# Every fourth wide weight split: the low part by an adding transfer instead of VectorE

## The chip, the cores and the metric

The kernel runs on one core of a Trainium2 chip. The metric is device microseconds for one execution; several executions are timed and their median is taken. TensorE (PE in the profile) multiplies, VectorE (DVE) and ScalarE (ACT) work on tiles in on-chip memory, GpSimd (POOL) does small side work, and SyncE (SP) issues loads from HBM.

## The reference, cut to what matters

A two-layer encoder over 256 tokens of width 1024. Each layer is a feed-forward block, a mixer (attention) and a second feed-forward block:

```python
def swiglu(h, w_gate, w_up, w_down):
    return (jax.nn.silu(h @ w_gate) * (h @ w_up)) @ w_down
...
    for layer in range(DEPTH):
        h = rms_norm(x, ffn1_norm[layer])
        x = x + 0.5 * swiglu(h, ffn1_w_gate[layer], ffn1_w_up[layer], ffn1_w_down[layer])
        h = rms_norm(x, mix_norm[layer])
        ...                       # even_mixer or odd_mixer
        h = rms_norm(x, ffn2_norm[layer])
        x = x + 0.5 * swiglu(h, ffn2_w_gate[layer], ffn2_w_up[layer], ffn2_w_down[layer])
    return rms_norm(x, final_norm)
```

All of it is float32. The feed-forward width is 2816, so the four blocks' gate, up and down matrices are most of the weights.

## The kernel before

**Two parts for every factor.** The matrix products run on a narrower float type (fp32r). Each weight tile `raw` is therefore split into a high part, `hi`, which is the weight rounded to that type, and a low part, `lo = raw - hi`, which is what the rounding dropped. The activations are split in the same way (`th`, `tl`). One product of a weight piece is three matmuls, in `mm`: activation high by weight high (L453), activation high by weight low (L454), activation low by weight high (L455). TensorE takes them in this order, so the low part is needed one matmul after the high part.

**Where parts are made.** ScalarE writes the high part from the raw tile (`high_part`, L461), VectorE subtracts and writes the low part (`low_part`, L464). A unit of work is a `Split`: a raw tile of 128 partitions by up to 1024 elements in two pieces (two column halves of one row block, or two row blocks of 512 or 384 columns). Its kinds are narrow (attention weights, one piece at a time), wide (most feed-forward weights, both pieces at once) and the sums of the Strassen-like products (`strassen`, `seven_gates`), which save one product in eight in some chunks and some down rows.

**Buffers.** Raw tiles of over 512 elements per partition come from a pool of three, filled by SP's loads in `load` (L366). High and low parts come from a pool of seven pairs. A pair is free when the last of its matmuls is done, and only then can ScalarE write the next high part into it.

**Stages.** The feed-forward blocks are stages 0, 2, 3 and 5. Each goes through six column chunks of 512 or 384: eight gate pieces for token tile 0, the same eight for token tile 1, then the up pieces likewise, and later the rows of the down matrix.

**What sets the order.** The order on each engine is written out by the program: it records instructions in the sequence in which Python issues them, and each engine runs its list in order. After each product `tick` runs waiting small tasks (SiLU, norms, transposes, each with a counted delay) and, at a rate set per stage, `supply`, which makes the next split's high part. `low` makes its low part at the next tick, or earlier when a product needs it. GpSimd's own list in the feed-forward blocks is nearly empty: two powers per stage (`rstd`, L473) that give the reciprocal root for the norm.

Of the kernel before, what the change touches and what calls it, by code (L numbers as in the profile page):

```python
# [12 lines left out]
AF = mybir.ActivationFunctionType  # L13
ALU = mybir.AluOpType
# [6 lines left out]
D = 1024  # L21
# [25 lines left out]
ODD_RATE = [0.51, 0.41, 0.51, 0.49, 0.51, 0.39, 0.49, 0.51]  # L47

HELD = 2

X_WAIT = 5
R_WAIT = 3
# [74 lines left out]
class Split:  # L127
# [3 lines left out]
    def __init__(self, raw, uses, first=False, narrow=False, kind="wp", then=None):  # L131
        self.raw, self.first, self.narrow, self.kind, self.then = raw, first, narrow, kind, then
        n = raw.shape[1]
        self.left = sum(uses[i % len(uses)] for i in range(n))
        self.parts, self.made = None, 0

    def step(self):

# [50 lines left out]
def pairs(stage):  # L189
    return [({"p": "plain", "s": "strassen"}[o[0]], int(o[1:])) for o in DOWN[stage].split()]  # L190
# [9 lines left out]
class Trunk:  # L200
# [4 lines left out]
    def __init__(self, ctx, tc, a, out):  # L205
        self.ctx, self.tc, self.nc, self.a, self.out = ctx, tc, tc.nc, a, out
        pool = lambda name, bufs, **kw: ctx.enter_context(tc.tile_pool(name=name, bufs=bufs, **kw))
        self.one = pool("one", 1)
        self.ph = None
        self.raw = pool("raw", RAWS)  # L210
        self.wp = pool("wp", FIT["wp"])

        self.two = pool("two", 2)
        self.acc = pool("acc", 1, space=PSUM)
        self.n = 0
        self.rate = RATE[0]
        self.tasks, self.last, self.last_v = [], [], [[], []]
        self.units, self.whole, self.queue, self.due, self.half = self.plan(), [], [], 0, None
        self.live = {kind: 0 for kind in FIT}

        self.hts = {}

# [65 lines left out]
    def plan(self):  # L288
# [16 lines left out]
        def ffn(n, l, stage):  # L305
# [15 lines left out]
            for i, (kind, pair) in enumerate(pairs(stage)):  # L321
                src = a[n + "_w_down"][l][2 * pair * P : 2 * (pair + 1) * P, :].rearrange("(k p) n -> p k n", p=P)
                uses = [2, 3 if stage == 5 and i >= len(pairs(stage)) - HELD else 2]
                yield [(slice(0, P), src)], 2, D, uses, "wide" if kind == "plain" else kind
# [31 lines left out]
    def load(self):  # L356
        unit = next(self.units, None)
        if unit is None:
            return
        pieces, nk, w, uses, kind = unit  # L360
        if nk * w > 512:
            raw = self.raw.tile([P, nk, w], F32, tag="raw", name=self.name("raw"))
        else:
            raw = self.t([P, nk, w], "raw", 2)
        for sl, src in pieces:
            self.nc.sync.dma_start(raw[sl], src)  # L366

        halves = lambda t: t.rearrange("p (a w) -> p a w", a=2)
        if kind == "strassen":
            self.coming(self.strassen(raw, halves))  # L370
        else:
            views = [halves(raw[:, k, :]) for k in range(nk)] if w == D else [raw[:, k : min(k + 2, nk), :] for k in range(0, nk, 2)]
            self.coming([Split(view, uses, n == 0, kind == "narrow") for n, view in enumerate(views)])

    def coming(self, splits):
        self.whole += splits
# [25 lines left out]
    def supply(self):  # L402

        self.low()
        if not self.whole:
            return
        split = self.whole[0]
        _, a, w = split.raw.shape
        if split.parts is None:
            if split.first:  # L410
                self.load()
            if split.kind == "wp":
                split.parts = [self.wp.tile([P, 2, 512], F32R, tag=n, name=self.name(n)) for n in ("hi", "lo")]
            else:
                split.parts = [self.t([P, 2, 512], n, FIT["sum"], F32R) for n in ("shi", "slo")]
            split.parts = [t[:, :a, :w] for t in split.parts]
            self.live[split.kind] += 1
        sl = slice(split.made, split.made + split.step())
        self.high_part(split.parts[0][:, sl], split.raw[:, sl])
        split.made = sl.stop  # L420
        self.half = (split, sl)
        if split.made == a:
            self.whole.pop(0)

# [204 lines left out]
    def ffn(self):  # L629
# [295 lines left out]
        order = [i for i, (kind, _) in enumerate(down) if kind == "strassen"]  # L925
        for i, (kind, pair) in enumerate(down[:-HELD]):
            if kind == "strassen":
# [10 lines left out]
        if self.next.n == 6:  # L938
            last = [self.t([P, 2, 512], "shi", FIT["sum"], F32R) for _ in range(NT)]
            self.last = [t.bitcast(F32).rearrange("p a w -> p (a w)") for t in last]  # L940
        held = [f for _, pair in down[-HELD:] for f in (2 * pair, 2 * pair + 1)]
        for f in held:
# [590 lines left out]
```

## Time and profile before

| | |
|---|---|
| Runs | 956.24, 956.25 and 956.81 us, median 956.25 us |
| Span of the profiled execution | 954.4 us, 1.85 us less than the median, which is the time around it |
| Instructions in the span | 13005 |
| VectorE's subtractions for low parts of weights (L464 `lo<-raw,hi`) | 388 in three sizes, 375.9 us busy |
| ScalarE's high parts (L461 `hi<-raw`) | 388, 320.5 us busy |
| Transfers | 171.65 MB, 180 GB/s mean |
| Transfers issued by GpSimd | none |

An engine's busy time is given with its share of the span; the idle time of an engine that nobody waits for costs nothing. TensorE's matmuls overlap their neighbours, so the time from one to the next is shorter than the duration in the row (some 0.23 us for 512 columns where the row says 0.39). In a timeline row stand the start, the time, the engine, the line, and what is written from what; x2 means two in a row, and a bracket holds the idle time before it and who ended it.

### The profile page before, as it was taken

The page shows a single profiled execution, that of the slowest core. Times are in us where ns is not written, and L with a number is a line of the kernel's source. Part 1 is how long each engine was busy: PE and PEld are TensorE (multiplying, and loading weights), DVE is VectorE, ACT ScalarE, POOL GpSimd, SP SyncE. Part 2 cuts the span into 40 slices and gives each one's busy share as a digit, 9 for nine tenths or more (in the row PEclk, how much of TensorE's full clock was granted, in tenths as well). Part 3 has the DMA queues.
Part 4 walks back from the last instruction along what each step waited for, and adds up shares of the span by engine and source line. Part 5 has one row for each costly group of instructions (what it writes and reads, how often), then busy time and mean ns, then how long its engine had stood idle before and what let it go on. Part 6 is the DMA issues. An engine that isn't in the chain of part 4 may idle for free.

```text
span 954.4 us, 13005 instructions
## 1 busy us (share of the span) xinstructions
PE 942.5 (99%) x4767; PEld 795.7 (83%) x4767; DVE 791.9 (83%) x1244; ACT 585.3 (61%) x1011; POOL 95.3 (10%) x152
## 2 busy tenths in 40 slices
PE   9999999999999999999999999999999999999997
PEld 6888998877778889988888899888878888889886
DVE  6989777788869998787988888889877697996797
ACT  7555555477777565655646456557877585556453
POOL 1130000073420000000100000006130000000001
PEclk9999999999999999999999999999999999999999
DMA  8846665644425654766456476564624365466461
GB/s 289 267 135 204 204 214 176 218 132 94 128 89 176 216 193 143 243 220 217 145 168 199 151 217 222 198 242 137 202 97 145 121 201 196 134 207 201 165 242 44
DMA packets 82752, 171.65 MB, mean 180 GB/s; under 512 B 4096, under 2 KB 25344, under 8 KB 82688
## 3 DMA queue, kind: packets, MB, share of 16 engines
q1 hardware_dynamic: 82112, 170.04, 53.7%
q8 instruction: 37, 0.61, 0.3%
q10 hardware_dynamic: 576, 0.79, 0.2%
q14 instruction: 27, 0.22, 0.1%
HBM read 169.76 MB, written 1.05 MB: 179 GB/s over the span
## 4 chain that ended last, share of the span: by engine, by line
PE 90%; DVE 4%; ACT 3%; issue 1%; DMA 1%; POOL 1%; SPq 0%; POOLq 0%; DVEq 0%; ACTq 0%
PE pj L453 13%; PE pj L455 12%; PE pj L454 12%; PE s L454 11%; PE s L455 11%; PE s L453 11%; PE tp L531 3%; PE o L454 2%; PE o L455 2%; PE o L453 2%; PE o L1006 2%; DVE lo L464 2%; PE tp L1085 1%; PE tp L453 1%; PE tp L454 1%; PE tp L455 1%
## 5 line engine op out<-in xcount | busy, mean ns | idle before, releaser
L464 DVE TENSOR_TENSOR lo<-raw,hi 128x1024 fp32r<-128x1024 f32 (+2 forms) x388 | 375.9, 991 | 66.0 <-ACT hi L461 64.0
L461 ACT ACTIVATE hi<-raw 128x1024 fp32r<-128x1024 f32 (+2 forms) x388 | 320.5, 862 | 81.2 <-PE s L455 22.2
L453 PE MATMUL pj<-hi,th 128*128 128x512 f32 (+1 forms) x431 | 164.6, 382 | 0.0
L454 PE MATMUL pj<-lo,th 128*128 128x512 f32 (+1 forms) x431 | 161.1, 374 | 0.1
L455 PE MATMUL pj<-hi,tl 128*128 128x512 f32 (+1 forms) x431 | 161.1, 374 | 0.0
L453 PE MATMUL s<-hi,th 128*128 128x512 f32 (+1 forms) x373 | 142.0, 381 | 0.2 <-ACT hi L461 0.2
L454 PE MATMUL s<-lo,th 128*128 128x512 f32 (+1 forms) x373 | 139.0, 373 | 0.3 <-DVE lo L464 0.2
L455 PE MATMUL s<-hi,tl 128*128 128x512 f32 (+1 forms) x373 | 138.8, 372 | 0.0
L455 PEld LDWEIGHTS pj<-hi,tl 128*128 128x128 f32 x431 | 80.9, 188 | 12.2
L453 PEld LDWEIGHTS pj<-hi,th 128*128 128x128 f32 x431 | 81.0, 188 | 11.4 <-issue 0.9
L454 PEld LDWEIGHTS pj<-lo,th 128*128 128x128 f32 x431 | 81.1, 188 | 10.9 <-DVE lo L464 0.5
L454 PEld LDWEIGHTS s<-lo,th 128*128 128x128 f32 x373 | 70.2, 188 | 11.3 <-DVE lo L464 2.3
L455 PEld LDWEIGHTS s<-hi,tl 128*128 128x128 f32 x373 | 70.0, 188 | 9.8
L453 PEld LDWEIGHTS s<-hi,th 128*128 128x128 f32 x373 | 70.1, 188 | 9.3 <-ACT hi L461 0.4
L473 POOL TENSOR_TENSOR rstd<-var,mhalf 128x1 f32<-128x1 f32 (+2 forms) x16 | 17.1, 1069 | 592.7 <-DVE var L471 457.6
L461 ACT ACTIVATE shi<-two 128x1024 fp32r<-128x1024 f32 x30 | 31.8, 1059 | 41.6 <-DVE two L382 41.5
L464 DVE TENSOR_TENSOR slo<-raw,shi 128x1024 fp32r<-128x1024 f32 x30 | 36.6, 1221 | 20.5 <-ACT shi L461 20.5
L461 ACT ACTIVATE g_h<-tp 128x384 fp32r<-128x384 f32 (+1 forms) x48 | 25.7, 538 | 45.2 <-DVE quarters L679 24.4
L461 ACT ACTIVATE shi<-raw 128x1024 fp32r<-128x1024 f32 x30 | 31.7, 1058 | 33.2 <-PE s L455 19.1
L453 PE MATMUL s<-hi,g_h 128*128 128x512 f32 (+1 forms) x131 | 52.0, 397 | 0.0
L455 PE MATMUL s<-hi,g_l 128*128 128x512 f32 (+1 forms) x131 | 51.0, 389 | 0.0
L454 PE MATMUL s<-lo,g_h 128*128 128x512 f32 (+1 forms) x131 | 50.9, 388 | 0.0
(473 smaller groups left out, 1669.2 us busy)
## 6 DMA issues: line engine op xcount, KB each, us to landing
raw<-in_ffn_w_down SPq DMA_DIRECT2D x44, 1024.0 KB, 5.1
raw<-in_ffn_w_up SPq DMA_DIRECT2D x20, 1024.0 KB, 5.2
raw<-in_ffn_w_gate SPq DMA_DIRECT2D x18, 1024.0 KB, 5.1
raw<-in_ffn_w_gate SPq DMA_DIRECT2D x27, 512.0 KB, 3.9
raw<-in_ffn_w_up SPq DMA_DIRECT2D x24, 512.0 KB, 4.9
raw<-in_ffn_w_gate SPq DMA_DIRECT2D x16, 768.0 KB, 4.6
raw<-in_ffn_w_up SPq DMA_DIRECT2D x16, 768.0 KB, 4.8
raw<-in_odd_w_qkv SPq DMA_DIRECT2D x12, 1024.0 KB, 5.3
```

What stands on the lines that cost most here:

```text
L453: mm(ps, h, wh, start=first, stop=False)
L454: mm(ps, h, wl, start=False, stop=False)
L455: mm(ps, l, wh, start=False, stop=last)
L461: self.nc.scalar.activation(hi, src, AF.Copy)
L464: self.nc.vector.tensor_tensor(lo, src, hi.bitcast(F32), op=ALU.subtract)
L473: nc.gpsimd.tensor_tensor(r[:, :n], v[:, :n], self.mhalf[:, :n], op=ALU.pow)
L531: self.nc.tensor.transpose(tb[:, i * P : (i + 1) * P], src[:, i * P : (i + 1) * P], self.ident)
L1006: self.nc.tensor.matmul(O[64 * s : 64 * s + 64, i * P : i * P + P], v(b0 + i, s, kc), pT[s][:, i, kc, :], start=(kc == 0), stop=(kc == 1),)
L1085: nc.tensor.transpose(tb[:, o : o + P], p[:, i, kc * P : kc * P + P], self.ident)
```

## The change

In the order of the program's loads every fourth plain wide split whose tile comes from one matrix in one piece (gate, up or down; not the chunks that load gate and up together) gets its low part in another way. ScalarE writes the high part as before and then, in the low part's place, the raw tile times -1 rounded to fp32r, which is the negated high part. A transfer issued by GpSimd then reads the same weights from HBM once more and adds them onto it. VectorE has no instruction for such a split.

```diff
+ADDED = 4
...
-        self.parts, self.made = None, 0
+        self.parts, self.made, self.again = None, 0, None
...
-            views = [halves(raw[:, k, :]) for k in range(nk)] if w == D else [raw[:, k : min(k + 2, nk), :] for k in range(0, nk, 2)]
-            self.coming([Split(view, uses, n == 0, kind == "narrow") for n, view in enumerate(views)])
+            cut = lambda t: [halves(t[:, k, :]) for k in range(nk)] if w == D else [t[:, k : min(k + 2, nk), :] for k in range(0, nk, 2)]
+            splits = [Split(view, uses, n == 0, kind == "narrow") for n, view in enumerate(cut(raw))]
+            if kind == "wide" and len(pieces) == 1:
+                for split, src in zip(splits, cut(pieces[0][1])):
+                    self.wide += 1
+                    if self.wide % ADDED == 0:
+                        split.again = src
+            self.coming(splits)
...
         split.made = sl.stop
-        self.half = (split, sl)
+        if split.again is None:
+            self.half = (split, sl)
+        else:
+            lo = split.parts[1][:, sl]
+            self.nc.scalar.activation(lo, split.raw[:, sl], AF.Copy, scale=-1.0)
+            self.nc.gpsimd.dma_start(lo, split.again, accum_op=ALU.add)
```

This touches 49 splits: 17 of gate weights, 18 of up weights and 14 of down weights. In the changed kernel the copies and transfers stand at L433 and L434, and the lines below have moved: high parts are at L474, subtractions at L477, the three matmuls at L466, L467 and L468.

How the lists of instructions change is seen at one tight place, in stage 3, the gate weights of the last chunk (384 columns). The rows name the operation, what is written and what it is made from, with the program's buffer numbers, which differ between the two kernels. ScalarE before:

```order
L461 ACTIVATE g_12_h_5637<-tp_5624 128x512
L461 ACTIVATE k12h_5652<-quarters_5603 128x512
L461 ACTIVATE hi_5655<-raw_5443 128x2x384
L461 ACTIVATE hi_5668<-raw_5464 128x2x384
L461 ACTIVATE hi_5678<-raw_5464 128x2x384
L461 ACTIVATE hi_5699<-raw_5486 128x2x384
```

ScalarE now:

```order
L474 ACTIVATE g_12_h_5668<-tp_5655 128x512
L474 ACTIVATE k12h_5683<-quarters_5634 128x512
L474 ACTIVATE hi_5686<-raw_5472 128x2x384
L433 ACTIVATE lo_5687<-raw_5472 128x2x384
L474 ACTIVATE hi_5700<-raw_5493 128x2x384
L474 ACTIVATE hi_5710<-raw_5493 128x2x384
```

The negated copy stands right behind its high part, ahead of the next split's. On VectorE at the same place, before:

```order
L687 TENSOR_TENSOR quarters_5603<-quarters_5603 128x128
L647 SCALAR_TENSOR_TENSOR glu_5647<-s_5587,rstd_4675,silu_5545 128x384
L464 TENSOR_TENSOR lo_5656<-raw_5443,hi_5655 128x2x384
L464 TENSOR_TENSOR k12l_5653<-quarters_5603,k12h_5652 128x512
L464 TENSOR_TENSOR lo_5669<-raw_5464,hi_5668 128x2x384
```

And now:

```order
L700 TENSOR_TENSOR quarters_5634<-quarters_5634 128x128
L660 SCALAR_TENSOR_TENSOR glu_5678<-s_5618,rstd_4701,silu_5575 128x384
L477 TENSOR_TENSOR k12l_5684<-quarters_5634,k12h_5683 128x512
L477 TENSOR_TENSOR lo_5701<-raw_5493,hi_5700 128x2x384
L477 TENSOR_TENSOR lo_5711<-raw_5493,hi_5710 128x2x384
```

One subtraction is gone and the rest has moved up. GpSimd's list at the beginning of stage 2, now (before, the two `rstd` stand side by side there and nothing follows in the stage):

```order
L486 TENSOR_TENSOR rstd_3035<-var_3033,mhalf_81 128x1
L434 DMA lo_3082<-in_ffn_w_gate 128x2x512
L486 TENSOR_TENSOR rstd_3126<-var_3124,mhalf_81 128x1
L434 DMA lo_3190<-in_ffn_w_up 128x2x512
L434 DMA lo_3474<-in_ffn_w_gate 128x2x512
```

A transfer's issue stands between the two powers; it waits in GpSimd's list for ScalarE's copy. The lists of TensorE and SP hold the same operations in the same order as before.

More of the change, by code (lines that the diff above doesn't have):

```diff
@@ L219, in __init__ @@
         self.live = {kind: 0 for kind in FIT}
+        self.wide = 0
         self.hts = {}
```

## The prediction

> **What bounds the kernel now.** I read the page first, for the engines' shares and the granted clock, then the groups by line and the waits, then short stretches of the timeline at the splits that the change touches.
>
> ```profile
> span 954.4 us, 13005 instructions
> PE 942.5 (99%) x4767; PEld 795.7 (83%) x4767; DVE 791.9 (83%) x1244; ACT 585.3 (61%) x1011; POOL 95.3 (10%) x152
> PEclk9999999999999999999999999999999999999999
> q1 hardware_dynamic: 82112, 170.04, 53.7%
> ```
>
> TensorE is the bound: it issues matmuls for all but 11.9 us of the span at the full clock, and part of those 11.9 us is the end, after its last matmul. VectorE, which the change relieves, is busy for 83%, but what counts is whether TensorE waits for it.
>
> ```profile
> PE s L454 <- DVE lo L464: 0.2, 1, 0.2
> PEld s L454 <- DVE lo L464: 2.3, 6, 0.5
> DVE lo L464 <- ACT hi L461: 64.0, 72, 2.2
> ```
>
> The columns are us in total, times, longest. For low parts TensorE's matmuls waited 0.2 us in all, and its weight loads, which overlap matmuls, 2.3 us. There is hardly anything to win: a low part that arrives earlier saves at most these, and I take 0.5 us. What the change can do is make low parts later.
>
> **The change, part by part.**
>
> ```profile
> L464 DVE TENSOR_TENSOR lo<-raw,hi 128x1024 fp32r<-128x1024 f32 x182 | 218.1, 1220 | 32.4 <-ACT hi L461 31.8
> L461 ACT ACTIVATE hi<-raw 128x1024 fp32r<-128x1024 f32 x182 | 186.6, 1053 | 53.1 <-PE pj L455 17.2 <-PE s L455 14.5 <-DMA raw<-in_ffn_w_up 7.4
> L464 DVE TENSOR_TENSOR lo<-raw,hi 128x768 fp32r<-128x768 f32 x64 | 59.2, 952 | 15.2 <-ACT hi L461 14.6
> L461 ACT ACTIVATE hi<-raw 128x768 fp32r<-128x768 f32 x64 | 51.2, 838 | 10.0 <-DMA raw<-in_ffn_w_up 5.3 <-PE s L455 2.8 <-PE pj L455 1.8
> ```
>
> The order of instructions has 49 such low parts, 33 of 1024 elements and 16 of 768. VectorE loses 33 x 1.220 + 16 x 0.952 = 55.5 us (792 to 736, nearly all beside TensorE's work). ScalarE gains as many copies: 33 x 1.053 + 16 x 0.838 = 48.2 us (585 to 633 of 954). These lie beside TensorE's work too, but each holds back the next ScalarE instruction by 1.05 us. I cost that at nothing, because at those places TensorE will already be standing still for the low part itself; without that cover it is at most 18 x 1.05 = 19 us, at the 18 tight places counted below. The queues get 33 x 0.524 + 16 x 0.393 = 23.6 MB more on 170.04 MB: their share of 53.7% becomes 61%, or 69% if reading the destination back counts as much again. The raw buffer is now let go by ScalarE's copy instead of VectorE's subtraction, and SP's queue of loads behind it is neither clearly earlier nor later: nothing. GpSimd issues 49 transfers, each waiting in its queue for ScalarE's copy; behind them stand only the reciprocal roots (rstd), two per stage, and GpSimd is 10% busy, so one of these is late by a copy at most: nothing.
>
> What remains is the path to the low part. Before, VectorE makes it in 1.22 us after the high part. Now it is a copy, a hand-over to GpSimd, an issue, and a transfer that must read the weights from HBM and the negated part from SBUF, add, and write back. No row shows a transfer that GpSimd issues, or one that adds; the nearest rows are these:
>
> ```profile
> raw<-in_ffn_w_down SPq DMA_DIRECT2D x44, 1024.0 KB, 5.1
> raw<-in_ffn_w_gate SPq DMA_DIRECT2D x27, 512.0 KB, 3.9
> raw<-in_ffn_w_gate SPq DMA_DIRECT2D x16, 768.0 KB, 4.6
> raw<-in_ffn_w_up SPq DMA_DIRECT2D x16, 768.0 KB, 4.8
> L473 POOL TENSOR_TENSOR rstd<-var,mhalf 128x1 f32<-128x1 f32 (+2 forms) x16 | 17.1, 1069 | 592.7 <-DVE var L471 457.6
> 76.00:125.00 49.00, 49.00 (x264) 45.11 (x263) 37.65 (x50) 29.43 (x44) 0.00 (x0) 1.00 0.63 209
> 330.00:395.00 65.00, 65.00 (x333) 57.95 (x332) 58.02 (x76) 38.04 (x56) 0.00 (x0) 1.00 0.59 192
> ```
>
> Low end: copy 1.05 + a plain 512 KB load 3.9 = 5.0 us, with the issue free and the addition free. High end: copy 1.05 + issue 1.07 + 5.1 for the doubled bytes + a whole 1024 KB load in front, 2.4 us at the 1.2 us per 512 KB by which the rows of 3.9 and 5.1 differ = 9.6, rounded to 10 us. I take 7.6 us: copy 1.05, issue 1.07 (GpSimd's own smallest instruction, the nearest row), 5.1 (as many bytes as 1024 KB are read), and 0.4 for meeting a load (the engines are 0.6 busy in the gate stretches, the last two rows; 0.6 x half of 1.2). For 768 elements: 0.84 + 1.07 + 4.7 + 0.3 = 6.9 us.
>
> The DMA page of the Trainium skill ("DMA: Bandwidth & Descriptors", Anatomy of one DMA) fits a GpSimd-issued transfer by 2.0 us plus bytes over 436 GB/s, 3.2 us for 512 KB; by it the path would be an estimated 4.3 us with the copy, and the sum below, counted in the same way, some 12 us instead of 55, 968 us in all. The trace's plain 512 KB loads take 3.9 us, more than the page's fit, and no run here shows an adding transfer.
>
> **How much time there is.** From the end of a high part to the first matmul that reads its low part, the time is read pair by pair from the timeline. The longest or shortest of each class (where a row says x2, the two together end at its end):
>
> ```profile
> 572.16 0.83 ACT L461 ACTIVATE hi<-raw 128x768 fp32r<-128x768 f32 x1
> 574.04 0.45 PE L454 MATMUL s<-lo,th 128*128 128x384 f32 x1
> 291.87 2.00 ACT L461 ACTIVATE hi<-raw 128x1024 fp32r<-128x1024 f32 x2
> 298.05 0.39 PE L454 MATMUL pj<-lo,th 128*128 128x512 f32 x1
> 37.94 2.01 ACT L461 ACTIVATE hi<-raw 128x1024 fp32r<-128x1024 f32 x2
> 47.22 0.39 PE L454 MATMUL pj<-lo,th 128*128 128x512 f32 x1
> 407.89 1.06 ACT L461 ACTIVATE hi<-raw 128x1024 fp32r<-128x1024 f32 x1 [0.51 <-PE s L455]
> 424.99 0.39 PE L454 MATMUL o<-lo,g_h 128*128 128x512 f32 x1
> ```
>
> Class A, 18 of the 49: from 1.05 us (574.04 - 572.99) to 4.18 (298.05 - 293.87), mean 2.73; 11 have 1024 elements. Class B, 12: up to 7.27 (47.22 - 39.95), mean 6.01. Class C, 19: 7.6 to 16.0 (424.99 - 408.95), mean 10.4, mostly down weights; these are hidden.
>
> If each place paid its full shortage: class A 11 x 7.6 + 7 x 6.9 - 18 x 2.73 = 82.8 us, class B 15.6 us over its places below the price, together 98 us. But a stall gives ScalarE and VectorE time to get ahead, where it is they that are late and not the buffer. The high part of the shortest case follows ScalarE's previous work without a gap, which itself waited for VectorE, so it can move up; in eight places of class B the high part starts within 0.4 us of the matmul that frees its buffer, as here, and cannot:
>
> ```profile
> 571.62 0.63 ACT L461 ACTIVATE k12h<-quarters 128x512 fp32r<-128x512 f32 x1 [1.34 <-DVE quarters L687]
> 576.60 0.85 ACT L461 ACTIVATE hi<-raw 128x768 fp32r<-128x768 f32 x1 [0.28 <-PE s L455]
> ```
>
> In class A the buffers had been free for 2.6 to 12.5 us before the high part began; the shortest and the longest of the 18, the freeing matmul and the high part:
>
> ```profile
> 93.21 0.39 PE L455 MATMUL pj<-hi,tl 128*128 128x512 f32 x1
> 96.19 0.83 ACT L461 ACTIVATE hi<-raw 128x768 fp32r<-128x768 f32 x1
> 762.15 0.39 PE L455 MATMUL pj<-hi,ot_10l 128*128 128x512 f32 x1
> 775.02 1.05 ACT L461 ACTIVATE hi<-raw 128x1024 fp32r<-128x1024 f32 x1
> ```
>
> With all of that lead used, 13 us of the 98 remain. Much of the late work waits for matmuls that a stall moves along with it, so all is too much; I take the middle, 55 us, since neither end has a row nearer to it. Sum: span 954.4 + 55 - 0.5 = 1008.9; the runs' median of 956.25 is 1.85 us above the span, so the time is 1011 us.
>
> **Rivals.**
>
> Hidden, or a small gain (the other side): the path is 5.0 us or less and the lead is used fully. Then the sum over the 49 places is 0 and the low parts never end a wait; the time is 956 less 0.5 to 2.5 us, the two rows of waits above. It decides only if both hold. Against it: class A's mean of 2.73 us is below even 5.0.
>
> Cheap transfer: the path is 5.0 us and half of the lead is used. The 49 places then sum to 41 us without lead and 0 with all, 20.5 in the middle: 977 us. For it: nothing in the trace says that an addition or GpSimd's issue costs time. Against it: the destination's bytes must be read too.
>
> The transfer is much slower than a copy: a price of 10 us at each place (the high end). Counted the same way that is 187 us without lead, 63 with all, 125 in the middle: 1081 us. For it: the addition has no row, and transfers meet loads.
>
> The clock falls: the end of the trace shows what a standstill does (columns: PE, PEld, DVE, ACT, POOL busy, then clock, DMA share, GB/s).
>
> ```profile
> 947.90 0.28 PE L455 MATMUL tp<-hi,g_l 128*128 128x128 f32 x1
> 947.60:951.50 3.90, 0.58 (x6) 0.43 (x4) 2.62 (x9) 1.58 (x2) 0.93 (x1) 1.00 0.36 134
> 951.50:954.00 2.50, 0.00 (x0) 0.00 (x0) 0.00 (x0) 0.00 (x0) 0.00 (x0) 0.52 0.56 210
> ```
>
> About 3.4 us after the last matmul the granted clock halves. A shortage of class A is 4.6 us on average before any lead, so between 9 and 18 stalls could reach that. If each costs another such stretch at half speed, 1.7 us of work is lost each time: 15 to 31 us, 1026 to 1042 us. Against it: the standstill must fall on 3.4 us without a single matmul, and half-used lead leaves most stalls near that limit. The clock page of the Trainium skill ("TensorE: Matmul & The Clock Gate", Part 1) says the clock halves after one idle window of about 3.4 us and returns after a busy one; the trace's end agrees on the fall, and no run here shows the return.
>
> **How the numbers follow.** Forecast as summed, 0.51; hidden with no measurable change, 0.05; a gain beyond what can be measured, 0.03; cheap transfer, 0.08; slow transfer, 0.19; clock, 0.14. A measurement of this kernel tells a change of about 0.2%, 1.9 us, from none. So slower has 0.51 + 0.08 + 0.19 + 0.14 = 0.92, same 0.05, faster 0.03. The range runs from the cheap transfer, 977 us, to the middle of the slow one, 1081 us. Outside lie the hidden cases (0.08) and about half of the cheap and of the slow transfers, some 2 in 10 in all.
>
> **What would show it.** Right: VectorE's subtractions lose 33 and 16; ScalarE shows 49 copies of 1.05 and 0.84 us; the transfers of 512 KB land 5 to 6 us after their issue; TensorE's low-part matmuls (the second of the three) wait for these transfers some 30 times, 40 to 70 us in all, longest about 6, in the gate and up stretches, hardly in the down products; TensorE's busy time stays at 942 us. Wrong: landings under 4 us or waits below 10 us mean the low price; landings of 8 us, or loads that land later than before, mean the slow one; slices of the granted clock below 9 mean the clock.

## The result

The changed kernel takes 1154.33 us (median of 4 runs, 1152.61 to 1161.28) against 956.53 us for the kernel before beside it: 1.2085 times the time, 95% interval 1.2069 to 1.21. The change costs 198 us.

### The profile after

The page's head, the row of the granted clock and the two queues that carry weights, of the changed kernel (1153.06 us as a run, span 1151.2):

```profile
span 1151.2 us, 13142 instructions
PE 999.0 (87%) x4767; PEld 833.4 (72%) x4767; DVE 746.8 (65%) x1195; ACT 631.2 (55%) x1060; POOL 140.6 (12%) x201
PEclk9689899999997989899999898899999988989998
q1 hardware_dynamic: 82112, 170.04, 45.3%
q0 software_dynamic: 11536, 23.60, 11.6%
```

The 196.8 us by which the span grew divide exactly. TensorE's idle time went from 954.4 - 942.5 = 11.9 us to 1151.2 - 999.0 = 152.2 us, that is 140.3 more; its busy time went from 942.5 to 999.0 us with the same 4767 matmuls, 56.5 more. The first part is waiting, as TensorE's rows of the waits say (total, times, longest):

```profile
PE pj L467 <- DMA lo<-in_ffn_w_gate: 43.4, 6, 8.0
PE s L467 <- DMA lo<-in_ffn_w_gate: 40.6, 8, 16.8
PE pj L467 <- DMA lo<-in_ffn_w_up: 33.5, 9, 7.5
PE o L467 <- DMA lo<-in_ffn_w_down: 14.3, 5, 4.8
PE s L467 <- DMA lo<-in_ffn_w_up: 9.2, 5, 2.4
```

Together 141.0 us in 33 waits, all for the adding transfer; no row has TensorE waiting for a high part or for VectorE's low parts of weights. How late these land is in the list of transfers (times, KB, median us from issue to landing):

```profile
lo<-in_ffn_w_down POOLq DMA_DIRECT2D x14, 512.0 KB, 8.7
lo<-in_ffn_w_up POOLq DMA_DIRECT2D x10, 512.0 KB, 8.4
lo<-in_ffn_w_gate POOLq DMA_DIRECT2D x9, 512.0 KB, 8.2
lo<-in_ffn_w_gate POOLq DMA_DIRECT2D x8, 384.0 KB, 7.4
lo<-in_ffn_w_up POOLq DMA_DIRECT2D x8, 384.0 KB, 7.7
```

The whole path at the tight place that the change's section showed, in the timelines of ScalarE, GpSimd and TensorE:

```profile
710.40 0.85 ACT L474 ACTIVATE hi<-raw 128x768 fp32r<-128x768 f32 x1
711.16 0.83 ACT L433 ACTIVATE lo<-raw 128x768 fp32r<-128x768 f32 x1
712.40 1.21 POOL L434 DMA_DIRECT2D lo<-in_ffn_w_gate  x1 [10.28 <-ACT lo L433]
716.45 0.34 PE L466 MATMUL s<-hi,th 128*128 128x384 f32 x1
719.88 0.44 PE L467 MATMUL s<-lo,th 128*128 128x384 f32 x1 [3.10 <-DMA lo<-in_ffn_w_gate]
```

From the high part's end at 711.25 the copy ends at 711.99, GpSimd begins 0.41 us later, and TensorE starts 7.48 us after that: 8.6 us. TensorE had its high part at 716.45 and stood for 3.1 us.

The second part, the longer busy time, is the clock. Around a wait of 2.43 us that ended at 481.13, stretch by stretch (busy PE, PEld, DVE, ACT, POOL, then clock, DMA share, GB/s):

```profile
478.60:481.10 2.50, 0.10 (x1) 0.00 (x0) 1.47 (x4) 0.80 (x3) 0.00 (x0) 1.00 0.89 304
482.00:485.30 3.30, 3.30 (x12) 3.30 (x11) 1.22 (x2) 0.90 (x2) 0.00 (x0) 0.50 0.00 0
485.40:488.00 2.60, 2.60 (x16) 2.60 (x16) 1.08 (x2) 2.25 (x3) 1.22 (x1) 1.00 0.40 65
```

Behind the standstill TensorE is busy all the time, but in the low stretch its matmuls of 384 columns start 0.32 us apart, where at the full clock they start 0.17 us apart. The mean granted clock of the whole span is 0.933. At 0.50 where it is low, that is 0.067 x 1151.2 / 0.5 = 154 us of low clock, part of it inside the standstills themselves.

### The profile page after: what moved, and what is told of

Read it like the earlier page. It is cut to its first block, busy times and chain, and to the rows that moved or that the text cites. A ratio compares the mean times of both kernels' runs of the same rounds, so it can differ in the third digit from the quotient of the medians.

```text
span 1151.2 us, 13142 instructions
## 1 busy us (share of the span) xinstructions
PE 999.0 (87%) x4767; PEld 833.4 (72%) x4767; DVE 746.8 (65%) x1195; ACT 631.2 (55%) x1060; POOL 140.6 (12%) x201
## 3 DMA queue, kind: packets, MB, share of 16 engines
q1 hardware_dynamic: 82112, 170.04, 45.3%
q0 software_dynamic: 11536, 23.60, 11.6%
HBM read 193.35 MB, written 1.05 MB: 169 GB/s over the span
## 5 line engine op out<-in xcount | busy, mean ns | idle before, releaser
L477 DVE TENSOR_TENSOR lo<-raw,hi 128x1024 fp32r<-128x1024 f32 (+2 forms) x339 | 324.2, 972 | 191.7 <-ACT hi L474 189.7
L474 ACT ACTIVATE hi<-raw 128x1024 fp32r<-128x1024 f32 (+2 forms) x388 | 323.3, 861 | 148.7 <-PE pj L468 83.3
L467 PE MATMUL pj<-lo,th 128*128 128x512 f32 (+1 forms) x431 | 173.4, 402 | 77.1 <-DMA lo<-in_ffn_w_gate 43.4
L467 PE MATMUL s<-lo,th 128*128 128x512 f32 (+1 forms) x373 | 147.7, 396 | 49.8 <-DMA lo<-in_ffn_w_gate 40.6
L466 PE MATMUL pj<-hi,th 128*128 128x512 f32 (+1 forms) x431 | 172.9, 401 | 0.0
L468 PE MATMUL pj<-hi,tl 128*128 128x512 f32 (+1 forms) x431 | 170.4, 395 | 0.0
L467 PEld LDWEIGHTS pj<-lo,th 128*128 128x128 f32 x431 | 87.4, 203 | 94.8 <-DMA lo<-in_ffn_w_gate 45.7
L466 PE MATMUL s<-hi,th 128*128 128x512 f32 (+1 forms) x373 | 149.2, 400 | 0.0
L468 PE MATMUL s<-hi,tl 128*128 128x512 f32 (+1 forms) x373 | 145.9, 391 | 0.0
L467 PEld LDWEIGHTS s<-lo,th 128*128 128x128 f32 x373 | 75.0, 201 | 65.0 <-DMA lo<-in_ffn_w_gate 43.3
L468 PEld LDWEIGHTS pj<-hi,tl 128*128 128x128 f32 x431 | 87.5, 203 | 13.1
L466 PEld LDWEIGHTS pj<-hi,th 128*128 128x128 f32 x431 | 86.6, 201 | 12.9 <-issue 0.9
L466 PEld LDWEIGHTS s<-hi,th 128*128 128x128 f32 x373 | 75.5, 202 | 10.1
L468 PEld LDWEIGHTS s<-hi,tl 128*128 128x128 f32 x373 | 75.0, 201 | 10.6
L477 DVE TENSOR_TENSOR g_l<-tp,g_h 128x384 fp32r<-128x384 f32 (+1 forms) x48 | 29.5, 616 | 59.8 <-ACT g_h L474 54.1
L434 POOL DMA_DIRECT2D lo<-in_ffn_w_gate x17 | 20.7, 1219 | 378.2 <-ACT lo L433 236.3
L474 ACT ACTIVATE g_h<-tp 128x384 fp32r<-128x384 f32 (+1 forms) x48 | 25.8, 538 | 64.0 <-PE tp L544 46.7
L477 DVE TENSOR_TENSOR slo<-raw,shi 128x1024 fp32r<-128x1024 f32 x30 | 36.7, 1222 | 27.2 <-ACT shi L474 27.2
L474 ACT ACTIVATE shi<-raw 128x1024 fp32r<-128x1024 f32 x30 | 31.7, 1058 | 41.0 <-PE s L468 25.6
L466 PE MATMUL s<-hi,g_h 128*128 128x512 f32 (+1 forms) x131 | 52.7, 402 | 0.0
L468 PE MATMUL s<-hi,g_l 128*128 128x512 f32 (+1 forms) x131 | 51.2, 391 | 0.0
L467 PE MATMUL s<-lo,g_h 128*128 128x512 f32 (+1 forms) x131 | 51.2, 391 | 0.0
```

The lines of the kernel that those rows point to most:

```text
L434: self.nc.gpsimd.dma_start(lo, split.again, accum_op=ALU.add)
L466: mm(ps, h, wh, start=first, stop=False)
L467: mm(ps, h, wl, start=False, stop=False)
L468: mm(ps, l, wh, start=False, stop=last)
L474: self.nc.scalar.activation(hi, src, AF.Copy)
L477: self.nc.vector.tensor_tensor(lo, src, hi.bitcast(F32), op=ALU.subtract)
```

## Experiments

The theory after the result: nothing but the waits for late transfers (141 us) and the clock behind them (56 us). The rivals: ScalarE's copies, the extra traffic, and GpSimd's issue. Ratios are against the kernel before, run beside each group.

### neg_only: the copies alone

```diff
-            self.nc.gpsimd.dma_start(lo, split.again, accum_op=ALU.add)
+            self.half = (split, sl)
```

> ScalarE's 49 negated copies alone; no transfer, and VectorE subtracts as before. Theory (the 198 us are waits for the transfers, 141 us, and the clock that falls after them, some 56 us): the copies are hidden, 955 to 962 us, TensorE's busy time stays at 942. Rival (ScalarE's 48 us of copies delay everything behind them on its queue): 975 us or more, with TensorE waiting for ScalarE's high parts.

962.18 us, ratio 1.0064 (1.0049 to 1.0079), just above what the theory allowed. TensorE's busy time is 943.5 us of a span of 959.7, so its idle time grew from 11.9 to 16.2; 3.3 us of it is waiting for VectorE's low parts, 0.2 before. So the copies are not the 198 us. The 6 us are not quite their price either: in this run VectorE writes the low part over the copy and waits for it (33.6 us in 31 places), which the changed kernel does not do. In the prediction the copies were put at nothing under cover, and at most 19 us without.

### aside: the transfers where nobody waits

```diff
+            kind = ("add_r", "add_f", "plain", "act_plain")[self.n_aside % 4]
+            aside = self.ph.tile([P, 2, 320], F32R if kind == "add_r" else F32, ...)
+            self.nc.scalar.activation(aside, part(split.raw), AF.Copy, scale=-1.0)
+            ...      # the transfer onto aside: GpSimd with or without the addition, or ScalarE's queue
+            self.half = (split, sl)
```

> In the first three feed-forward stages the transfers go into a scratch tile that nobody reads (two rows of 320 elements per partition), in turn as an addition onto the kernel's narrow type, an addition onto float32, a plain load issued by GpSimd, and the same plain load issued from ScalarE's queue; VectorE makes every low part as before. Theory (waiting is what costs, and it is the addition that makes the landing late): 955 to 963 us; additions land 6.5 to 7.5 us after their issue, plain loads by GpSimd 4 to 5, by ScalarE 3.5 to 4.5. Rival 1 (whatever GpSimd issues is slow): the plain loads of GpSimd land as late as the additions, 6.5 us or more. Rival 2 (the change to the narrow type is slow): additions onto float32 land as early as plain loads. Rival 3 (the extra traffic slows the loads of weights): 975 us or more.

The four kinds, by the list of transfers (columns as above):

```profile
add_r<-in_ffn_w_up POOLq DMA_DIRECT2D x7, 320.0 KB, 7.7
add_f<-in_ffn_w_gate POOLq DMA_DIRECT2D x6, 320.0 KB, 6.6
plain<-in_ffn_w_up POOLq DMA_DIRECT2D x6, 320.0 KB, 4.7
act_plain<-in_ffn_w_gate ACTq DMA_DIRECT2D x6, 320.0 KB, 3.5
add_f<-in_ffn_w_down POOLq DMA_DIRECT2D x3, 320.0 KB, 7.2
plain<-in_ffn_w_down POOLq DMA_DIRECT2D x3, 320.0 KB, 5.4
act_plain<-in_ffn_w_down ACTq DMA_DIRECT2D x3, 320.0 KB, 6.2
add_r<-in_ffn_w_down POOLq DMA_DIRECT2D x2, 320.0 KB, 8.1
```

The addition costs about 2 us (4.7 to 6.6, 5.4 to 7.2); that the same engine issues it does not explain it, since GpSimd's plain loads land early (rival 1 falls). Additions onto float32 do not land as early as plain loads, so rival 2 falls too. Adding onto the narrow type is later again, by about 1 us (6.6 to 7.7, 7.2 to 8.1), which is within what matrices of one kind differ by, so whether the type costs anything is not shown. GpSimd against ScalarE's queue is open here: 1.2 us in the gate and up rows, the reverse in the down rows, with three transfers each.

The time was missed: 972.5 us, ratio 1.0174 (1.0157 to 1.0191), where up to 963 was expected. The rows of the waits name a cause of my own making:

```profile
ACT plain L442 <- DMA add_f<-in_ffn_w_gate: 14.4, 2, 13.3
```

There is one scratch tile, and ScalarE stood 13.3 us for it in one place, until the transfer before had landed. So this run tells landings, and nothing about the cost of traffic (rival 3). The page of the changed kernel says something about that: the packets of the kernel's own loads took 45.3% of 1151.2 us, 521 us of the sixteen engines, against 53.7% of 954.4, 512 us, before, so with the extra traffic beside them they took 2% longer in all.

### neg_first: the transfer starts 1.05 us earlier

```diff
+        if split.again is not None:
+            lo = split.parts[1][:, sl]
+            self.nc.scalar.activation(lo, split.raw[:, sl], AF.Copy, scale=-1.0)
+            self.nc.gpsimd.dma_start(lo, split.again, accum_op=ALU.add)
         self.high_part(split.parts[0][:, sl], split.raw[:, sl])
...
-        else:
-            ...      # the same three lines, behind the high part
```

> The negated copy and the transfer stand ahead of the high part on ScalarE, so the transfer starts 1.05 us earlier (0.84 for 768 elements). Theory: each of some 31 waits for a transfer is shorter by about that, 141 us become 108 to 118, and some stretches of low clock go too: 1105 to 1130 us. Rival (the transfers are late because they queue behind each other and behind the loads, not because they are issued late): waits and time stay within 10 us of 1154.

1117.15 us, ratio 1.1684 (1.1661 to 1.1708), as the theory expected. TensorE waits for transfers:

```profile
PE s L467 <- DMA lo<-in_ffn_w_gate: 39.3, 8, 16.8
PE pj L467 <- DMA lo<-in_ffn_w_gate: 38.0, 6, 7.4
PE pj L467 <- DMA lo<-in_ffn_w_up: 27.6, 9, 7.4
PE o L467 <- DMA lo<-in_ffn_w_down: 7.0, 4, 3.5
PE s L467 <- DMA lo<-in_ffn_w_up: 2.5, 4, 1.0
```

In all 114.4 us in 31 waits, 27 us less, and the busy time fell from 999.0 to 986.5. A path shorter by one copy is worth 37 us: the length of the path is what counts.

### pool_plain: the addition left out

```diff
-            self.nc.gpsimd.dma_start(lo, split.again, accum_op=ALU.add)
+            self.nc.gpsimd.dma_start(lo, split.again)
```

> The transfers are plain loads onto the low part, issued by GpSimd as in the change and waited for as in the change; the addition is left out, so the low part holds the weight itself. Theory (the addition doubles the time of every packet, 327 ns against 159 for 4096 bytes): the landing falls from 8.2 to about 5.3 us, the waits from 141 to 55 to 75 us, the clock part with them to 15 to 30, and the time to 1035 to 1065 us. Rival (GpSimd's issue and the queueing among loads make the landing late): 7 us or more to landing and 1110 us or more.

1075.58 us, ratio 1.1254 (1.1204 to 1.1303), between the ranges of theory and rival. The queue and two of its transfers:

```profile
q0 software_dynamic: 11536, 23.60, 6.8%
lo<-in_ffn_w_down POOLq DMA_DIRECT2D x14, 512.0 KB, 6.4
lo<-in_ffn_w_gate POOLq DMA_DIRECT2D x9, 512.0 KB, 6.2
```

The same packets and bytes took 6.8% of a span of 1070.3 us, 73 us of the sixteen engines, instead of 11.6% of 1151.2, 134 us: with the addition they take 1.83 times as long. The Trainium skill says of the add in a ReduceScatter between cores that it needs two source reads, which double the read traffic ("Collectives: The Full Stack", The bandwidth ceiling); the 1.83 here is in line with that, though no run counts the reads. The landing improves by 2.0 to 2.3 us, TensorE's waits fall from 141 to 83 us, and the time by 79 of the 198 us. The rest of the loss stays without any addition: some 6.3 us to landing for 512 KB, with copy and hand-over ahead of it, is more than most of the tight places have (class A 2.73 us on average, class B 6.01). In the same run SP's plain loads of 512 KB landed 3.9 to 5.1 us after their issue; why GpSimd's take longer is not shown.

### skip_second and skip_two: what stands ahead on GpSimd

The longest wait, 16.8 us, belongs to the second transfer. ScalarE's copy for it and GpSimd's timeline there, in the changed kernel:

```profile
38.09 1.05 ACT L433 ACTIVATE lo<-raw 128x1024 fp32r<-128x1024 f32 x1
...
23.82 1.36 POOL L434 DMA_DIRECT2D lo<-in_ffn_w_up  x1 [3.97 <-ACT lo L433]
24.76 0.72 POOL L1432 CAST m<-mats 128x128 bf16<-128x128 f32 x1
52.33 0.40 POOL L1435 CAST m<-far 128x256 bf16<-128x256 f32 x1 [26.84 <-DMA far<-in_c_far]
...
57.00 1.12 POOL L434 DMA_DIRECT2D lo<-in_ffn_w_gate  x1
```

The attention's table work (`tables`) stands between the first two transfers and waits 26.8 us for its input, a small load. The copy for the second transfer was done at 39.1 us; it was issued at 57.0. Two runs take the second, then the second and the third transfer out of the change:

```diff
-                    if self.wide % ADDED == 0:
+                    if self.wide % ADDED == 0 and self.wide != 2 * ADDED:
```

```diff
-                    if self.wide % ADDED == 0:
+                    if self.wide % ADDED == 0 and self.wide > 3 * ADDED or self.wide == ADDED:
```

> The second of the 49 splits gets its low part from VectorE; the other 48 as in the change. Its transfer was issued 18 us after its copy, because it stood behind the table work on GpSimd that waits for a small load. Theory: the wait of 16.8 us goes, and half of the 20 us of low clock behind it: 1125 to 1137 us. Rival (the pause only lets other work catch up, and the next waits grow by as much): 1147 us or more.

> The second and the third of the 49 splits get their low parts from VectorE. Theory (GpSimd's table work, which waits for the small load far, holds whatever transfer stands behind it): with none between the first transfer and the end of that work, the wait of 16.8 us and the 1.6 us go, and most of the 20 us of low clock after 48 us, so 1120 to 1135 us, clearly below skip_second's 1142.9. Rival (time lost there is found again elsewhere): 1140 us or more.

Without the second, 1142.88 us, between the ranges of theory and rival. Of the gain of 11 us, the waits give only 3.8 (137.2 us in all), because the next one grew, as the rival said:

```profile
PE pj L467 <- DMA lo<-in_ffn_w_up: 43.3, 9, 10.2
```

It was 33.5 with a longest of 7.5: the third transfer was now the one behind the table work. Without both, 1130.99 us, inside the range: the waits are 121.5 us, 19.5 less, and the busy time 994.5, 4.5 less. So 23 us of the 198 hang on these two transfers. A small part of that is the ordinary shortage there: TensorE came to the second at 46.07, so that with a free queue, 0.41 us of hand-over and 8.2 to landing it would have waited for an estimated 1.7 us, and the third wait was 1.6 us in the changed kernel.

### fill: the clock

TensorE multiplies a tile of zeros during the standstill, in 33 places, as often as fits the wait measured there: 642 times in all by the list in the program, not the 594 of the expectation.

```diff
+STILL = {1: 34, 2: 76, 3: 7, ...}      # how many, by the transfer's number
...
         mm(ps, h, wh, start=first, stop=False)
+        for _ in range(split.still):
+            mm(ps, self.zero_r, wh, start=False, stop=False)
+        split.still = 0
         mm(ps, h, wl, start=False, stop=False)
```

> At 33 of the 49 splits TensorE multiplies a tile of zeros by the split's high part, added onto the same sum, between the first and the second matmul of the split's first product, as many times (3 to 76, 594 in all, 0.22 us each) as would fill the standstill measured there in the changed kernel. Theory (a standstill lets the clock fall, and that is the 56 us by which TensorE's busy time grew): the granted clock stays full through the filled places, the waits nearly vanish, the real matmuls take their 0.39 us again, and despite 131 us of useless matmuls the time falls by 40 to 60 us, to 1095 to 1115. Rival (the clock is not set by the standstill but by the kernel's load, or the busy time grew from something else): the low clock remains, and the time is 1150 us or more, since every filler that overshoots adds to it.

```profile
span 1124.4 us, 14427 instructions
PE 1089.6 (97%) x5409; PEld 918.3 (82%) x5409; DVE 745.6 (66%) x1195; ACT 630.1 (56%) x1060; POOL 140.6 (13%) x202
PEclk9999999999999999999999999999999999999999
```

The clock stays full (mean 0.992 against 0.933), and with 642 matmuls more the kernel is 29 us faster, 1124.88 us. So the standstills cause the low clock, and the rival falls. The 642 take some 0.22 us each, 141 us; without them the busy time is 948, against 942 before and 999 in the change. That the gain is 29 and not the 40 to 60 expected has its reason in the sum: fillers and idle time together are 141 + 34.8 = 176 us, 24 more than the 152 us of idle time in the change. The likely reason, which no run isolates: at half the clock TensorE comes later to the next late transfer, and so waits less for it; at the full clock it comes on time and waits. By this run, of the 56 us about 30 are a net cost of the clock, and the rest would be waiting otherwise.

### ample and ample2: only where there is time

The transfer at 16 other splits, no two neighbours, each with 11 us or more between high part and first use in the kernel before; then the same without two of them.

```diff
-ADDED = 4
+ADDED = {39, 42, 44, 48, 50, 87, 90, 92, 94, 101, 103, 105, 142, 159, 161, 189}    # ample2: without 48, 50
...
-                    if self.wide % ADDED == 0:
+                    if self.wide in ADDED:
```

> The adding transfer at 16 other splits, no two neighbours, at each of which the kernel before left 11.3 us or more between the high part's end and the low part's first matmul; the path measured in the changed kernel is 9.7 us. VectorE loses 19 us of work. Theory (only waiting costs): no wait of TensorE for a transfer beyond 1 us in all, clock full, 955 to 959 us, no gain either, because TensorE did not wait for VectorE. Rival 1 (the doubled packets slow the weights' loads): 962 us or more. Rival 2 (VectorE's relief is worth something): 953 us or less.

959.77 us, ratio 1.0039 (1.0026 to 1.0052), just above the theory's range. No wait for a transfer is left, but ScalarE and TensorE show one new one each:

```profile
179.24 1.16 ACT L474 ACTIVATE hi<-raw 128x512 fp32r<-128x512 f32 x2 [6.73 <-DMA raw<-in_even_w_in]
189.19 0.66 PE L522 MATMUL tp<-mats,x 128*128 128x128 f32 x4 [2.38 <-DVE x L597]
```

Beside transfers 48 and 50, 2.8 us apart, the attention's weights landed 8.1 to 12.1 us after their issue, where they took 5.1 to 6.8 before. A high part was late, VectorE behind it, and TensorE at the end. Here the traffic costs time, as rival 1 said, though less than the 962 us that it forecast.

> ample without its two transfers at the end of the first down product (14 remain). In ample the loads of the attention's first weights, issued between those two, landed after 8.1 to 12.1 us instead of 5.1 to 6.8, one high part came late, and one wait of 2.4 us with a 3.4 us stretch of low clock stood for its 4 us. Theory (that one collision is all that ample lost): 955 to 957 us, no wait for a transfer, no low clock before the end. Rival (small losses everywhere): 958 us or more. Other rival (VectorE's 17 us of relief show once nothing collides): 954 us or less.

Without those two: 955.99 us, ratio 0.9999 (0.9990 to 1.0008), and the page's row of the engines is that of the kernel before but for VectorE:

```profile
PE 942.1 (99%) x4767; PEld 795.9 (83%) x4767; DVE 776.9 (81%) x1230; ACT 598.1 (63%) x1025; POOL 108.8 (11%) x166
```

VectorE lost 15 us of work and the kernel is neither faster nor slower. No version tried here beats the kernel before.

## Why the prediction was wrong in size

The direction was right. The step that failed is the price of one late low part, 7.6 us where the path took 9.7 to 10.2; beside it stood two costs that the sum left out: work ahead of a transfer on GpSimd, put at nothing, and the clock, put into a rival. The signs that the prediction named for the slow transfer and for the clock all came: landings of 8 us, loads that land later (512 KB of gate weights 4.3 us instead of 3.9), and slices of the granted clock below 9.

**Right.** Slower, because TensorE does not wait for VectorE and the low parts come late; ample2 shows both halves of it. VectorE lost 45 us and ScalarE gained 46 (55 and 48 forecast), the traffic grew by the 23.60 MB of the sum, TensorE waited 33 times where some 30 were forecast, and the down products waited least, 14.3 of 141 us.

**The price of the path was too low.** For 512 KB the sum had copy 1.05, issue 1.07, transfer 5.1 and 0.4 for meeting loads, 7.6 us. Measured: copy 1.05, hand-over 0.4, and 8.2 to 8.7 from the start of the issue to the landing, so 9.7 to 10.2 us. The terms mis-sized are the transfer, 5.1 by the row of a plain 1024 KB load, and the hand-over, which had no term. The row was no good neighbour: pool_plain shows that half as many bytes, issued by GpSimd and not added, already take 6.2 to 6.4 us, where the sum's parts for that are 1.07 + 3.9 + 0.4 = 5.4, and that the addition brings 2.0 to 2.3 more, where the sum had 5.1 - 3.9 = 1.2. The fit of the Trainium skill ("DMA: Bandwidth & Descriptors", Anatomy of one DMA), by which 512 KB take an estimated 3.2 us, is farther off still.

**The middle between no lead and all lead came out, in part by luck.** At the price of 10 us, the slow transfer's, that rule gave 125 us. Without the second transfer's 16.8 us, most of which has another cause, the measured waits are 141.0 - 16.8 = 124 us. But the prediction had no row for the middle, and the waits were counted with the clock low in places: in fill, at the full clock, fillers and idle time came to 24 us more. How far ScalarE and VectorE really got ahead in a standstill was not measured.

**The clock was made a rival, and it is a consequence.** The forecast took the case of the slow transfer and the case of the clock as alternatives with chances of 0.19 and 0.14. They came together, and fill shows why: it is the waits that let the clock fall. The size was wrong too, 15 to 31 us against 56.5. Against the clock the prediction held that a standstill must fall on 3.4 us without a single matmul, and that one low stretch of 3.4 us follows. Both failed: a wait of 2.43 us was enough for one, and the clock is low for longer around long waits, as at the first two (the same columns as above):

```profile
28.00:38.20 10.20, 6.17 (x15) 4.82 (x16) 3.56 (x5) 1.07 (x2) 0.00 (x0) 0.50 0.33 66
49.00:68.90 19.90, 6.05 (x16) 4.88 (x17) 1.69 (x2) 2.68 (x5) 5.71 (x23) 0.50 0.32 80
```

These waits ended at 32.03 and 62.85 us, so 4 and 14 us of the two stretches lie inside the standstill, where a low clock costs nothing, and some 6 us of each behind it. Over the whole kernel, each of the 19 waits of 3.05 us or more had a low stretch, of the eight between 2.43 and 2.76 us four had one, and none of the six of 1.66 us or less. What decides is told at the end.

**A queue was counted by what stands behind, not by what stands ahead.** The prediction says that behind a transfer on GpSimd stand only the reciprocal roots, and costs the queue at nothing. Ahead of the second transfer stands the table work, and skip_two puts that place at 23 us, the third transfer with it. The waits of the kernel before had it in a row (total, times, longest):

```profile
POOL m L1422 <- DMA far<-in_c_far: 23.1, 1, 23.1
```

Together, 125 for the waits at 10 us, 16.8 for the second transfer and 56.5 for the clock are 198 us, against a span that grew by 196.8. The last two are taken from the same profile as the span, so the sum tests only the 125, and with the reserve above.

## What to carry to other kernels

An engine that is busy for 83% is worth relieving only if the rows of the waits say that the bound engine waits for it; if not, its work is cheaper there than on any path that is longer. A hand-over to a transfer is priced from the whole chain (copy, hand-over, issue, landing beside other traffic) and set against the time at each place of use, and an instruction added to an idle queue can still stand behind work that waits for something else. When waits of some 2.4 us or more, the shortest here with a low clock behind it, are forecast on TensorE, the clock belongs into the same sum and not into a case of its own.

## What the runs showed of the hardware

- An adding transfer keeps the sixteen engines busy 1.83 times as long as a plain one of the same packets (134 against 73 us for 23.60 MB), and lands 2.0 to 2.3 us later at 512 KB.
- The granted clock fell to 0.50 after a standstill of 2.43 us, less than the idle window of about 3.4 us that the Trainium skill gives ("TensorE: Matmul & The Clock Gate", Part 1); after another of 2.45 us, ending at 493.74, it stayed full. The trace says why. All 47 changes of the clock in the changed kernel lie on one grid of 3.413 us. Cut along this grid, the first standstill falls into one stretch and the second into two:

```profile
478.53:481.94 3.41, 0.98 (x6) 0.81 (x5) 1.47 (x4) 1.40 (x3) 0.00 (x0) 1.00 0.71 242
488.77:492.18 3.41, 2.52 (x15) 2.20 (x13) 1.55 (x3) 0.11 (x1) 0.00 (x0) 1.00 1.01 251
492.18:495.59 3.41, 1.85 (x12) 1.81 (x13) 0.07 (x1) 0.86 (x3) 0.00 (x0) 1.00 0.96 343
```

  TensorE is busy for 0.29 of the first, and for 0.74 and 0.54 of the others. Over all stretches of the grid at the full clock, the next one was at half the clock behind each of the 24 in which TensorE was busy for 0.41 or less, and at the full clock behind each of the 268 with 0.49 or more. From a low stretch it came back behind each of the 23 that were busy for 0.84 or more, and behind none of the 21 with 0.83 or less. In pool_plain the first border lies between 0.45 and 0.52; in neg_first one stretch of 0.50 was followed by a low one and one of 0.49 was not, so the border is known only to a few hundredths.
- Beside two adding transfers issued 2.8 us apart, five loads of the attention's weights landed 8.1 to 12.1 us after their issue in ample, instead of 5.1 to 6.8 in the kernel before. Why these suffer so much more than the feed-forward weights was not tested.
